# Block 2's mixing stages: TensorE issues in the order of the program

## The chip, the cores and the metric

The kernel runs on one core of a Trainium2 chip. The metric is the device time of one execution in microseconds (us), and the median of several executions is given. A core has five engines that matter here, each with a queue of its own that it works through in order: TensorE (PE in the profile; its weight loads stand apart as PEld), VectorE (DVE), ScalarE (ACT), GpSimd (POOL) and SyncE (SP), which issues the DMA transfers.

## The reference

Two blocks are computed, one behind the other. Block 1 is a diffusion-type transformer on 512 latent and 256 context tokens. Block 2 takes 512 tokens of width 1024 through two layers. What matters here is the first half of each of these layers, the mixing: the normalised input is projected once into many parts, three kinds of mixing run on these parts, their results are put side by side and projected back.

```python
for l in range(DEPTH):
    hn = rms_norm_2(h, attn_norm[l])
    proj = hn @ w_in[l]
    p_a = proj[..., :RW_IN]
    p_b = proj[..., RW_IN:RW_IN + RET_IN]
    p_c = proj[..., RW_IN + RET_IN:]
    ...
    y_a, v_first = rwkv7_mixer(p_a, ...)
    y_b = retention_mixer(p_b, positions)
    y_c = mla_mixer(p_c, positions, mla_q_norm[l], mla_kv_norm[l], mla_w_q_up[l], mla_w_kv_up[l])
    mix = jnp.concatenate([y_a.astype(h.dtype), y_b.astype(h.dtype), y_c.astype(h.dtype)], axis=-1)
    h = h + mix @ w_out[l]
```

- RWKV: four heads of width 64 in two pairs, a recursion over the tokens with data-dependent decay. The kernel computes it in chunks of 64 tokens: inside a chunk a triangular system is solved by doubling, and a state is handed on from chunk to chunk. The output is normalised per head and multiplied by a gate.
- MLA: causal softmax attention of eight heads with keys and queries of width 96 (64 plus 32 with rotary position), whose queries, keys and values come from normalised low-rank latents.
- Retention: four heads of width 64 in two pairs, causal with a fixed decay per head, in chunks of 128 tokens, normalised per head and multiplied by a gate.

A SwiGLU follows as the second half of the layer. Products of projections are made from three matmuls each, on a high and a low part (`whi`, `wlo`; `hh`, `hl`) of both operands.

## The kernel before, in words

The kernel is written as a Python program whose calls append instructions, in the order in which they are made, to the queues of the engines. That is the order of the source. A build step then plans each engine's queue anew: it simulates the engines with estimated costs, and an engine takes whichever of its instructions is ready first. So the order of issue on an engine can differ from the source, wherever nothing that an instruction needs stands against it. A call `tc.keep_in_program_order(ins)` binds an instruction to the one appended just before it on the same engine, so that the build can't exchange the two.

Block 2's mixing (`block2`, L1881 to L1898) has two parts per layer.

The weave. `rwkv` is a Python generator that yields a number whenever the next instruction of its own has to wait for another engine: the gap in microseconds that other work could fill. `weave` adds gap / `STEP` (1.4) to a credit and takes one step of a second generator, the filler, for every whole credit. A filler step is a few matmuls of a projection (six matmuls, two of the eight input tiles times three products), or the vector work behind one. The filler is `mla_inputs` (projections that MLA needs; L1588) and behind it `ret_inputs` and `retention` (L1557, L1689), of which `mla_inputs` itself takes some steps. Two places are of interest: `scale` in `mla_inputs`, which sums squares over tokens with eight small matmuls on a tile `acc` (`token_sums`), and `head_rstd_steps` (L1196 to L1220), which ends each RWKV pair and each retention pair. It does eight small matmuls on squares, then a chain of small VectorE instructions for one over the root (`rsqrt`, L225 to L230, on a tile `smlR` or `smlL`), yields 3.2, and then does sixteen small matmuls that spread the result over rows. Behind it L1552 to L1554 finish the pair on VectorE, and the result is stored.

MLA. When the weave is through, `mla` (from L1893 on) handles eight heads of four query blocks. It casts queries and keys into `qk` (L1770, ScalarE; L1771, VectorE), makes scores, softmax, transposes and products with the values. After each block it takes steps of what is left of the filler, at a rate that spreads them over the stage. What is still left at its end is run at L1895. MLA's pool of tiles takes the place of RWKV's, which is closed by then. Behind the mixing stage come the output products on `mh` and `ml`.

All matmuls go through `mm` (L159) and all transposes through `turn` (L163), so these two lines are TensorE's lines in the profile, and one goes by the tiles' names.

Of the kernel before, what the change touches and what calls it, by code (L numbers as in the profile page):

```python
# [39 lines left out]
class Seg:  # L40


    def __init__(self, key, off, n):
        self.key, self.off, self.n = key, off, n
        self.v = 0 if key == "lat" else 1
# [12 lines left out]
class Kern:  # L58
    def __init__(self, tc, d, out, ctx, V):
        self.tc, self.nc, self.d, self.out = tc, tc.nc, d, out  # L60
        self.ctx, self.V = ctx, V
        nc = self.nc
        self.uid = 0
        E = ctx.enter_context
        self.const = E(tc.tile_pool(name="const", bufs=1))
        self.wp = E(tc.tile_pool(name="wp", bufs=2))
        self.tmp = E(tc.tile_pool(name="tmp", bufs=2))
        self.dram = E(tc.tile_pool(name="dram", bufs=1, space=DRAM))
        c = self.const
        self.vec = c.tile([128, d["vec"].shape[1]], F32, name="vec")  # L70
        nc.sync.dma_start(out=self.vec, in_=d["vec"])
        self.cf = c.tile([128, d["cf"].shape[1]], F32, name="cf")
        nc.sync.dma_start(out=self.cf, in_=d["cf"])
        self.ident = self.cf[:, 0:128]
        self.ones = self.cf[:, 128:129]
        self.bones = self.cf[:, 129:131]
        self.nhalf = self.cf[:, 131:139]
        self.identb = c.tile([128, 128], BF16, name="identb")
        nc.vector.tensor_copy(self.identb, self.ident)
        self.mge = c.tile([128, 128], BF16, name="mge")  # L80
        self.mle = c.tile([128, 128], BF16, name="mle")
        for o, m in ((0, self.mge), (128, self.mle)):
            t = self.tm(128)
            nc.sync.dma_start(out=t, in_=d["cm"][:, o:o + 128])
            nc.vector.tensor_copy(m, t)
        self.ahead = []
        self.banks = {}
        self.lo = "vector"
        self.lb = itertools.cycle("lb")
        self.pend = []  # L90
        self.stream = "L"


    def pool(self, es, name, side=None):
# [61 lines left out]
        self.nc.vector.tensor_tensor(lo, x, hi.bitcast(F32), op=ALU.subtract)  # L156

    def mm(self, out, l, r, start, stop):
        self.nc.tensor.matmul(out, l, r, start=start, stop=stop)  # L159

    def turn(self, out, x):

        self.nc.tensor.transpose(out, x, self.ident)  # L163

    def proj(self, chunks, H, seg, ps):
        for _ in self.proj_steps(chunks, H, seg, ps):
# [1421 lines left out]
    def mla_inputs(self, l, pool, H, bc, rs, tab, dst, acc, bl, other):  # L1588
# [70 lines left out]
        for j in range(2):  # L1659
            yield from latent("kv", 16, 2, j)  # L1660
        turn = rotary()
        next(turn)
        rl = scale("kv", 2)
        yield
# [157 lines left out]
    def block2(self):  # L1822
# [28 lines left out]
        for l in range(2):  # L1851
# [3 lines left out]
            with ExitStack() as es:  # L1855
                es_l = ExitStack()
                self.psum(es, r=4)
                self.psum(es_l, "right", l=2, b=2)
                rp = self.pool(es, "rw")
                bc, slots = X["lat"][7], X["lat"][:7]  # L1860
                ahead = [self.w2proj(l, 6, H)]
                st = self.token_sums(accs, "r")
                rs = self.inv_sqrt(st[:, 0:4], 1.0 / 1024)
                if l == 0:
                    s2 = self.sml(4)
                    nc.vector.tensor_tensor(s2, st[:, 4:8], rs, op=ALU.mult)
                    nc.vector.tensor_tensor(s2, s2, rs, op=ALU.mult)
                    r2 = self.inv_sqrt(s2, 1.0 / 1024)
                    r1, rs = rs, self.one(self.const, [128, 4], F32, "rst")
                    nc.vector.tensor_tensor(rs, r1, r2, op=ALU.mult)  # L1870
                ahead += [self.w2proj(l, j, H) for j in (2, 3)]
                self.spread(rs, "r", bc)
                r, k, v, mis = self.rw_inputs(l, rp, H, bc, slots, ahead)
                es_r, es_rets, es_mix, es_ps = (ExitStack() for _ in range(4))
                retp = self.pool(es_r, "ret", "right")
                mix = [{"lat": [None] * KD} for _ in range(2)]
                with ExitStack() as er:
                    self.order_w(self.orders(l))
                    self.filler = self.counted(self.streamed("L", self.retained(l, retp, es_rets, H, bc, rs, tab_r, mix)))
                    first = self.streamed("L", self.mla_inputs(l, self.pool(er, "fill", "right"), H, bc, rs, tab_m, sm, *self.acc2, self.filler))  # L1880
                    self.weave(self.streamed("R", self.rwkv(l, rp, r, k, v, mis, mixd, vf, C2)), itertools.chain(first, self.filler))  # L1881
                    self.run(first)
                self.lo = "vector"
# [6 lines left out]
            with ExitStack() as es:  # L1890
# [2 lines left out]
                self.mla(l, self.pool(es, "mla"), slots, sm, mixd)  # L1893
                self.stream = "L"
            self.run(self.filler)  # L1895
            es_rets.close()
            es_r.close()
            es_ps.close()  # L1898
# [11 lines left out]
            if l == 0:  # L1910
                b1 = self.bank()
                self.spread_into(r1, b1)
                for k_ in range(KD):
                    x = X["lat"][k_]
# [254 lines left out]
```

## Time and profile before

| what | value |
|---|---|
| median of 3 runs | 3359.4 us (3358.96 to 3359.47) |
| the profiled execution | 3356.98 us |
| its span in the trace | 3355.1 us |
| mixing stage of layer 0 | 1968.4 to 2213.2 us, MLA from 2118.0 |
| mixing stage of layer 1 | 2673.9 to 2920.5 us, MLA from 2832.5 |

The profiled execution is 2.4 us under the median, and 1.9 us of it lie around the span. A timeline gives, for each group of like instructions of one engine, the start, the duration, engine, line, operation, tiles (out<-in), sizes, and in brackets the idle time before it and what ended that. The granted clock of TensorE stands in windows as PEclk; 1.00 is 2.4 GHz.

### The profile page before, as it was taken

To read this page: it belongs to the slowest core of one execution; us is meant where nothing else is said; L and a number is where in the kernel's file an instruction comes from. 1 tells how busy PE (TensorE), PEld (TensorE's weight loads), DVE (VectorE), ACT (ScalarE), POOL (GpSimd) and SP (SyncE) were. 2 spreads that over 40 slices of the span, in tenths; PEclk is the share of its full clock that TensorE was granted. 3 is DMA by queue.
4 is the path that set the end of the run, shared out by engine and by line. 5 is a ranking of instruction groups with operands and counts; after the bars stand their busy time and mean duration, and the time that the engine had idled before them with its cause. 6 is when DMAs were issued, how large, how long until landed. Compare 5 with 4: busy or idle time off the path is not lost. (4 is left out here: it accounts for less than half of the span.)

```text
span 3355.1 us, 48877 instructions
## 1 busy us (share of the span) xinstructions
PE 3281.4 (98%) x19412; PEld 2737.1 (82%) x19412; DVE 1923.1 (57%) x3336; ACT 1233.3 (37%) x2192; POOL 398.6 (12%) x362
## 2 busy tenths in 40 slices
PE   8999999999999999999999999999999999999998
PEld 4888888888888888888888877778888867788887
DVE  7667765666444567757333466774434566754343
ACT  3566632421212346734222432542222332632222
POOL 4231100100000101101000211121101101121001
PEclk8999999999999999999999999999999999999999
DMA  6433373334434243353232323433233323422332
GB/s 217 133 111 123 113 255 128 107 121 135 128 120 133 81 135 101 97 182 118 94 91 98 123 70 103 131 97 94 90 99 98 105 76 102 130 94 94 90 99 82
DMA packets 137533, 385.86 MB, mean 115 GB/s; under 512 B 17428, under 2 KB 29204, under 8 KB 137304
## 3 DMA queue, kind: packets, MB, share of 16 engines
q1 hardware_dynamic: 133976, 372.15, 35.3%
q0 software_dynamic: 3328, 10.57, 1.0%
q8 instruction: 153, 2.51, 0.3%
q14 instruction: 76, 0.62, 0.1%
HBM read 331.56 MB, written 43.76 MB: 112 GB/s over the span
## 5 line engine op out<-in xcount | busy, mean ns | idle before, releaser
L140 ACT CAST whi<-raw 128x1024 fp32r<-128x1024 f32 (+4 forms) x432 | 434.8, 1008 | 1266.7 <-PE b L159 836.1
L141 DVE TENSOR_TENSOR wlo<-raw,whi 128x1024 fp32r<-128x1024 f32 (+4 forms) x427 | 509.2, 1193 | 379.7 <-ACT whi L140 358.2
L159 PE MATMUL b<-hh,whi 128*128 128x512 f32 (+1 forms) x1760 | 686.5, 390 | 0.0
L159 PE MATMUL b<-hl,whi 128*128 128x512 f32 (+1 forms) x1760 | 682.1, 388 | 0.8 <-POOL hl L251 0.8
L159 PE MATMUL b<-hh,wlo 128*128 128x512 f32 (+1 forms) x1760 | 681.7, 387 | 0.0
L159 PEld LDWEIGHTS b<-hh,whi 128*128 128x128 f32 x1760 | 331.0, 188 | 75.5 <-issue 4.8
L159 PEld LDWEIGHTS b<-hh,wlo 128*128 128x128 f32 x1760 | 330.8, 188 | 73.7 <-issue 0.7
L159 PEld LDWEIGHTS b<-hl,whi 128*128 128x128 f32 x1760 | 331.0, 188 | 71.5 <-POOL hl L251 1.2
L159 PE MATMUL b<-ah,whi 128*128 128x512 f32 (+1 forms) x864 | 316.8, 367 | 0.0
L159 PE MATMUL b<-al,whi 128*128 128x512 f32 (+1 forms) x864 | 316.5, 366 | 0.0
L159 PE MATMUL b<-ah,wlo 128*128 128x512 f32 (+1 forms) x864 | 316.3, 366 | 0.0
L159 PEld LDWEIGHTS b<-ah,whi 128*128 128x128 f32 x864 | 163.1, 189 | 28.2
L159 PEld LDWEIGHTS b<-ah,wlo 128*128 128x128 f32 x864 | 163.0, 189 | 28.0
L159 PEld LDWEIGHTS b<-al,whi 128*128 128x128 f32 x864 | 163.1, 189 | 27.8
L948 DVE TENSOR_TENSOR tm<-tm,b 128x512 f32<-128x512 f32 (+1 forms) x112 | 70.0, 625 | 198.8 <-PE b L159 192.8
L409 DVE SCALAR_TENSOR_TENSOR wlo<-raw,silb 128x1024 f32<-128x1024 f32 x128 | 157.6, 1232 | 45.3 <-DMA raw<-in_ada1b 24.5
L159 PE MATMUL l<-hh,whi 128*128 128x512 f32 (+1 forms) x472 | 176.7, 374 | 0.7 <-DVE stB L698 0.3
L159 PE MATMUL l<-hl,whi 128*128 128x512 f32 (+1 forms) x472 | 173.5, 368 | 0.0
L159 PE MATMUL l<-hh,wlo 128*128 128x512 f32 (+1 forms) x472 | 172.9, 366 | 0.0
L509 DVE TENSOR_TENSOR pt<-t,pt 128x384 fp32r<-128x384 f32 (+2 forms) x272 | 131.0, 511 | 36.5 <-ACT pt L508 34.9
L159 PE MATMUL b<-hc,whi 128*128 128x256 f32 x800 | 141.5, 279 | 0.0
L468 DVE TENSOR_REDUCE st<-S 128x1 f32<-128x768 f32 (+2 forms) x160 | 121.6, 763 | 33.5 <-PE S L159 32.7
(561 smaller groups left out, 5766.2 us busy)
## 6 DMA issues: line engine op xcount, KB each, us to landing
raw<-in_wgu SPq DMA_DIRECT2D x92, 512.0 KB, 3.3
raw<-in_w2gu SPq DMA_DIRECT2D x88, 512.0 KB, 3.4
raw<-in_ada1b SPq DMA_DIRECT2D x48, 512.0 KB, 3.3
raw<-in_w2in SPq DMA_DIRECT2D x38, 512.0 KB, 3.6
raw<-in_ada0b SPq DMA_DIRECT2D x32, 512.0 KB, 3.9
raw<-in_wg SPq DMA_DIRECT2D x32, 512.0 KB, 3.4
raw<-in_w2d SPq DMA_DIRECT2D x32, 512.0 KB, 3.5
raw<-in_wd SPq DMA_DIRECT2D x24, 512.0 KB, 3.5
```

The source lines that it names most:

```text
L140: self.nc.scalar.copy(hi, raw)
L141: getattr(self.nc, self.lo).tensor_tensor(lo, raw, hi.bitcast(F32), op=ALU.subtract)
L159: self.nc.tensor.matmul(out, l, r, start=start, stop=stop)
L409: nc.vector.scalar_tensor_tensor(junk, raw, 0.5, self.silb[:, v], op0=ALU.mult, op1=ALU.mult, accum_out=m[:, w, k, v:v + 1])
L468: nc.vector.tensor_reduce(nm, S[:, lo:hi], axis=AX.X, op=ALU.max, negate=True)
L509: nc.vector.tensor_tensor(o, src, h.bitcast(F32), op=ALU.subtract)
L948: nc.vector.tensor_tensor(b, th, pu, op=ALU.mult)
```

## The change

For the length of both mixing stages, every matmul and transpose is bound to the one appended before it: TensorE's queue is the source's order from the weave on until the last step of filler behind MLA. The switch `given` is off everywhere else. The other engines' queues are still planned by the build.

```diff
@@ class Kern, __init__ @@
         self.stream = "L"
+        self.given = False
@@ mm, turn @@
     def mm(self, out, l, r, start, stop):
-        self.nc.tensor.matmul(out, l, r, start=start, stop=stop)
+        self.queued(self.nc.tensor.matmul(out, l, r, start=start, stop=stop))
 
     def turn(self, out, x):
 
-        self.nc.tensor.transpose(out, x, self.ident)
+        self.queued(self.nc.tensor.transpose(out, x, self.ident))
+
+    def queued(self, ins):
+
+        if self.given:
+            self.tc.keep_in_program_order(ins)
@@ block2, each layer @@
                     first = self.streamed("L", self.mla_inputs(l, self.pool(er, "fill", "right"), H, bc, rs, tab_m, sm, *self.acc2, self.filler))
+                    self.given = True
                     self.weave(self.streamed("R", self.rwkv(l, rp, r, k, v, mis, mixd, vf, C2)), itertools.chain(first, self.filler))
                     self.run(first)
...
             self.run(self.filler)
+            self.given = False
             es_rets.close()
```

## Rows read from the trace of the kernel before

**Rows 1.** The page: span, and busy time of each engine.

```profile
span 3355.1 us, 48877 instructions
...
PE 3281.4 (98%) x19412; PEld 2737.1 (82%) x19412; DVE 1923.1 (57%) x3336; ACT 1233.3 (37%) x2192; POOL 398.6 (12%) x362
```

**Rows 2.** Windows: weave, hand-over and end of MLA, both layers.

```profile
core 0: us, PE busy (x) PEld busy (x) DVE busy (x) ACT busy (x) POOL busy (x), PEclk, DMA share, GB/s
1968.40:2118.00 149.60, 143.91 (x1588) 108.87 (x1587) 102.67 (x272) 41.74 (x74) 16.98 (x22) 0.97 0.28 82
2118.00:2145.50 27.50, 25.58 (x181) 21.67 (x180) 22.54 (x43) 15.37 (x38) 5.13 (x4) 1.00 0.38 113
2174.40:2213.20 38.80, 35.22 (x305) 28.44 (x303) 27.73 (x81) 22.36 (x60) 6.61 (x6) 0.96 0.42 130
2673.90:2832.50 158.60, 149.42 (x1602) 111.44 (x1601) 105.14 (x275) 44.73 (x77) 21.50 (x25) 0.97 0.27 81
2832.50:2861.30 28.80, 28.23 (x211) 24.61 (x209) 21.66 (x48) 16.30 (x41) 4.26 (x4) 1.00 0.38 117
2884.40:2920.50 36.10, 32.97 (x304) 27.22 (x301) 27.22 (x81) 22.07 (x60) 6.47 (x6) 1.00 0.44 140
```

**Rows 3.** Timeline of TensorE: token sums, layer 0, then layer 1.

```profile
2052.40 0.40 PE L159 MATMUL b<-hh,whi 128*128 128x512 f32 x1
...
2053.57 0.40 PE L159 MATMUL b<-hh,wlo 128*128 128x512 f32 x1
2054.88 1.05 PE L159 MATMUL b<-cf,acc 128*128 128x1 f32 x8 [0.91 <-DVE acc L208]
...
2698.63 1.05 PE L159 MATMUL b<-cf,acc 128*128 128x1 f32 x8 [1.48 <-DVE acc L208]
```

**Rows 4.** Timeline of TensorE: hand-over of layer 0.

```profile
2117.97 0.40 PE L159 MATMUL b<-hh,whi 128*128 128x512 f32 x1
...
2122.36 1.09 PE L159 MATMUL r<-cf,smlR 128*64 128x128 f32 x16 [0.49 <-DVE smlR L230]
...
2129.97 0.48 PE L159 MATMUL l<-qk,qk 96*128 96x128 f32 x2
```

**Rows 5.** Timeline of VectorE and ScalarE: hand-over of layer 0.

```profile
2116.66 0.17 DVE L1207 TENSOR_SCALAR smlR<-r 128x8 f32<-128x8 f32 x1 [2.74 <-PE r L159]
...
2122.06 0.15 DVE L230 SCALAR_TENSOR_TENSOR smlR<-smlR,smlR 128x8 f32<-128x8 f32 x1
2123.50 0.75 DVE L1552 SCALAR_TENSOR_TENSOR s<-s,vec,r 128x512 f32<-128x512 f32 x1 [1.28 <-PE r L159]
...
2125.07 0.69 DVE L1554 TENSOR_TENSOR s<-s,r 128x512 f32<-128x512 f32 x1
...
2128.77 1.13 ACT L1770 CAST qk<-x 96x512 fp32r<-96x512 f32 x2
```

**Rows 6.** Timeline of TensorE: hand-over of layer 1.

```profile
2832.49 0.39 PE L159 MATMUL b<-hh,whi 128*128 128x512 f32 x1
...
2836.32 1.09 PE L159 MATMUL r<-cf,smlR 128*64 128x128 f32 x16
```

**Rows 7.** Windows: two of the stretches at a lower granted clock.

```profile
2079.20:2082.60 3.40, 3.40 (x12) 2.69 (x9) 2.14 (x5) 0.00 (x0) 0.86 (x3) 0.50 0.56 130
2922.30:2929.10 6.80, 6.48 (x14) 4.74 (x15) 4.55 (x6) 2.33 (x5) 1.55 (x1) 0.50 0.24 77
```

**Rows 8.** Timeline: end of layer 0's MLA, VectorE and TensorE.

```profile
2205.25 0.17 DVE L1202 TENSOR_TENSOR smlL<-b,r 128x8 f32<-128x8 f32 x1 [1.22 <-PE b L159]
...
2208.77 1.05 PE L163 MATMUL t<-cf,x 128*128 128x128 f32 x4 [0.92 <-ACT x L472]
...
2209.42 0.17 DVE L1210 TENSOR_TENSOR smlL<-smlL,rst 128x8 f32<-128x8 f32 x1
...
2211.87 1.34 PE L159 MATMUL o<-mpt,mv 128*128 128x256 f32 x8
```

**Rows 9.** Timeline of TensorE: first products behind each mixing stage.

```profile
2215.30 0.97 PE L159 MATMUL b<-mh,whi 128*128 128x512 f32 x3 [1.15 <-ACT mh L155]
...
2922.61 0.79 PE L159 MATMUL b<-mh,whi 128*128 128x512 f32 x1 [2.14 <-ACT mh L155]
```

## The prediction

> **What bounds the kernel now.** I read the page first. It gives the span, and TensorE (PE) as busy for nearly all of it, with VectorE (DVE) at 57% and every other engine below that [rows 1]. So the time is the time of TensorE's queue: work on other engines costs only where TensorE waits for it, and a wait that nothing fills is paid in full. The edit acts in Block 2's two mixing stages (1968.4 to 2213.2 us and 2673.9 to 2920.5 us), so I cut these into three stretches each, by windows: the weave, the hand-over to MLA, and the end of MLA [rows 2]. The reader is to see there how much TensorE idles: 149.60 − 143.91 = 5.69 us and 158.60 − 149.42 = 9.18 in the weaves, 27.50 − 25.58 = 1.92 and 28.80 − 28.23 = 0.57 at the hand-overs, 38.80 − 35.22 = 3.58 and 36.10 − 32.97 = 3.13 at the ends. Whatever order is used there, the most that better cover could win is 24.1 us.
>
> Then I read TensorE's timeline of both stages against the order of the source. It is nearly the source's own order already: only some fifty places in about 1,540 instructions of a layer differ. The change matters at those alone, and most of them are of one kind: filler that the build put ahead of an instruction that waits for another engine. I took them in turn.
>
> **The change, part by part.** It removes and adds no instruction, no transfer and no semaphore that a result needs. It fixes the order in which TensorE issues; the other engines' queues are still planned, against that order.
>
> *Token sums* (`scale`, called twice a layer). The eight small matmuls on `acc` wait for VectorE's sum of squares. Before, filler of the projection that follows was moved ahead of them: in layer 0 six matmuls, from 2052.40 to 2053.57, and even so the sums still waited 0.91 us [rows 3]. The other three places have 2, 8 and 6. They are spaced by (2053.57 − 2052.40) / 5 = 0.234 us. In source order they stand behind the sums, so the wait is longer by their time: 22 × 0.234 = **5.1 us**. VectorE's `acc` comes no sooner for it, since nothing before it has moved. The bounds are 0, if the planner brings L208 forward, and 5.1.
>
> *Hand-over, first wait.* `head_rstd_steps` of the second RWKV pair traces eight sums on TensorE, a chain of twelve small VectorE operations, `yield 3.2`, and then sixteen small matmuls (L1218) on the chain's result `smlR`. By the source the 3.2 of credit buys two filler steps, and the second is a rope without matmuls: six matmuls stand in between. The six are through at 2117.97, and from there to 2122.36 before ran sixteen matmuls of filler that the source places in MLA [rows 4]. In source order this filler is not there, and TensorE waits for `smlR`, which is written at 2122.06 + 0.15 [rows 5]: 2122.36 − 2117.97 = 4.39 us. In layer 1 the same stretch is 2836.32 − 2832.49 = 3.83 us [rows 6]. The low bound: twelve operations at about 0.2 us each (start to start, as from 2116.66) make 2.4 us, so if VectorE ran nothing between them the wait would be about 1.1 us. The planner ranks VectorE's queue by the same estimates as before, so I keep the measured chain.
>
> *Hand-over, second wait.* Behind those sixteen the next TensorE instructions of the source are MLA's first scores, and these need `qk`. Before, over fifty filler matmuls stood there, to 2129.97 [rows 4]. Now the chain is: L1552 to L1554 on VectorE, from 2123.50 to 2125.07 + 0.69 = 2125.76; they are the last to use RWKV's pool, whose place the MLA pool takes; then ScalarE's two casts, 1.13 us [rows 5]: first scores at about 2126.9. The sixteen end near 2123.4, so the wait is 3.5 to 3.6 us, and the same in layer 1. If the casts also had to wait until the store of `s` has landed, 2 to 3 us more per layer; if the pools do not overlap, nothing.
>
> So the hand-over gains 4.39 + 3.6 = 8.0 and 3.83 + 3.6 = 7.4 us of waits, against 1.92 and 0.57 that it has now and that go into them: 6.1 + 6.9 = **13.0 us** (bounds 4 and 19).
>
> *Clock.* There are six stretches in the two stages and just behind them in which the granted clock is 0.50, the lower of its two levels (1.2 GHz); the first and the last are [rows 7]. They are 3.4 or 6.8 us long, three of each, and each comes after waits of TensorE. Half of such a stretch is lost: 2.55 us in the mean. Each hand-over will now have two waits of about 4 us close together, where before it ran at 1.00 [rows 2]. I take one stretch for each: **5.1 us** (bounds 0 and 10). The Trainium skill ("TensorE: Matmul & The Clock Gate", section "Loop structure matters more than you think") speaks against the change here: matmuls should follow one another while the other engines' work is overlapped, and a wait between matmuls lets the clock fall. The trace agrees, with 0.50 behind the 2.14 us wait of [rows 9]; by that rule the term stays, and without it the sum would be 5.1 us less.
>
> *End of MLA.* Retention's two norms go through the same function on the last filler. In source order only about 2.1 us (first) and 0.65 us (second) of TensorE work, by the durations that these instructions have in the trace, lie between its sums and its sixteen matmuls, and the VectorE chain takes from 2205.25 to 2209.59 [rows 8]: 4.3 us, with other work between its operations, or 14 × 0.2 = 2.9 without. That gives waits of about 2.0 and 2.9 us, and the last eight matmuls on values (1.34 us [rows 8]) lose the sixteen as cover: 1.3 more, 6.2 us per layer. Something is won here, though: the stretch's own idle goes into it, save 1.90 of 3.58 and 0.56 of 3.13 that wait for ScalarE whatever the order (0.92 of it is in [rows 8]), and the next stage's wait for `mh` (1.15 and 2.14 us) [rows 9] is worked off meanwhile. So 6.2 − 1.68 − 1.15 = 3.4 and 6.2 − 2.57 − 2.14 = 1.5: **4.9 us** (bounds −5 and 12).
>
> *Inside RWKV.* The doubling levels and the state recursion keep the places they have, and the few filler matmuls that change sides of a hop do it both ways: 0 (bounds −2 and +3).
>
> The sum: 5.1 + 13.0 + 5.1 + 4.9 = 28.1 us. On the profiled execution's 3357.0 that is 3385.1; this execution lies 2.4 us under the median of the runs, so the median comes to 3387.5. I write **3387 us**.
>
> **The rivals.** 0.2% (6.7 us) is about what a measurement can tell from no change.
>
> *Heavier.* The first scores also wait for the landing of RWKV's store, the half clock lasts 6.8 us at each hand-over or comes back at the ends, and the end's terms are near their upper bound: 13.0 goes to 18, 5.1 to 8, 4.9 to 9, in all some 40 us, **3400**. For it: casts into `qk` stand at 2128.77, after that landing could have been. Against it: nothing in the page shows which of the two they waited for.
>
> *No measurable change.* The waits come, but the planner, seeing TensorE stand at `smlR` and at `qk`, puts VectorE's chain and the casts first: 2.4 us of chain leaves 1.1 instead of 4.4, casts start at once, the clock stays up, and the end's gain (−5) pays for the rest: 5.1 + 4 + 0 − 5 = 4 us, **3364**. Against it: in both layers VectorE ran filler's work between the chain's operations, and nothing in the edit ranks that work lower.
>
> *Faster.* Mechanism: filler that before ran early is missing later, and in source order it stands in the hops of RWKV and at MLA's end for which it was written. Its price at full effect: the weaves' idle 5.69 + 9.18 = 14.9, their four stretches at half clock 10.2, and the avoidable end waits 1.68 + 1.15 + 2.57 + 2.14 = 7.5, together −32.6. It would have to pay for the token sums and the hand-over, 18.1: net −14.5, **3345**. It decides from 24.8 us, three quarters of the whole, on. For it: half-clock stretches do sit in the weave. Against it: in the weave only 22 matmuls are out of place by more than a hop, so there is hardly any stolen filler to give back.
>
> That the edit does nothing is excluded by the places of [rows 3] and [rows 4], which source order doesn't allow.
>
> **How the numbers follow.** The likeliest case (3372 to 3394) 0.62; heavier (3394 to 3406) 0.17; no measurable change 0.12; faster 0.09. Thus faster 0.09, within 0.2% 0.12, slower 0.79. The range leaves out the faster case and the tail of the heavier: 3360 to 3403; the likeliest case's own is 3372 to 3394.
>
> **What would show it.** In the profile after: the same counts of instructions; TensorE waiting for `smlR` (L230) about 4 us and then for `qk` 3.6 us at each hand-over; the sums on `acc` waiting about 2 us and more instead of 0.91 and 1.48 [rows 3]; a clock below 1.00 in the hand-over windows; a wait for `smlL` at the end and a smaller one for `mh`. I am wrong if TensorE's idle time in the mixing stages grows by less than 10 us, or if the weaves get shorter.

## The result and the profile after

The changed kernel takes 3408.86 us in the median of 4 runs (3405.53 to 3411.57), against 3359.18 (3358.58 to 3359.47): a ratio of 1.014, 95% interval 1.0127 to 1.0152, or +49.7 us. The prediction had the direction and about half the size: +28, and 3387 in a range from 3360 to 3403. The profiled execution took 3411.57 us, 54.6 more than the one of before, and it is the one taken apart here.

In the changed kernel's listing TensorE's matmuls stand at L160 (L159 before) and the other lines of the argument six lines lower: L214 for L208, L236 for L230, L1216 for L1210, L1777 for L1771. The page gives the same counts of instructions on every engine, so no work came or went (the total in the first line, which also has instructions that are in no engine's count, differs by 15):

```profile
span 3409.8 us, 48862 instructions
...
PE 3293.3 (97%) x19412; PEld 2752.7 (81%) x19412; DVE 1922.5 (56%) x3336; ACT 1233.4 (36%) x2192; POOL 397.7 (12%) x362
```

TensorE's busy time rose by 3293.3 − 3281.4 = 11.9 us [rows 1] with the same matmuls, and the granted clock below is lower. The rest of the 54.7 us of span, some 43 us, is idle time. To see where, I put each matmul of the one trace beside its like in the other and cut the changed kernel's at the same matmuls. By layer, the windows are the weave, the hand-over, the end of MLA, and the first output products behind it. The last cut of layer 1 fell among like matmuls that the two orders place differently, so the tail of MLA stands in the window behind (278 matmuls against 304), and these two windows are to be read together:

```profile
core 0: us, PE busy (x) PEld busy (x) DVE busy (x) ACT busy (x) POOL busy (x), PEclk, DMA share, GB/s
1968.04:2128.13 160.09, 147.87 (x1588) 113.71 (x1586) 103.24 (x271) 41.53 (x73) 17.09 (x22) 0.93 0.26 76
2128.13:2162.67 34.54, 26.42 (x181) 22.57 (x180) 22.05 (x46) 16.16 (x41) 5.13 (x4) 0.90 0.36 105
2191.49:2237.60 46.11, 34.16 (x305) 28.49 (x304) 29.77 (x83) 23.56 (x63) 7.31 (x6) 0.91 0.37 110
2237.60:2258.55 20.95, 20.95 (x83) 16.82 (x83) 11.24 (x18) 5.22 (x9) 1.28 (x1) 0.87 0.16 51
2699.43:2866.22 166.79, 150.77 (x1601) 113.81 (x1599) 106.05 (x274) 45.84 (x79) 20.62 (x25) 0.95 0.26 76
2866.22:2904.02 37.80, 30.85 (x211) 27.10 (x210) 23.10 (x51) 17.70 (x44) 4.11 (x4) 0.86 0.32 98
2928.31:2968.70 40.39, 30.34 (x278) 26.12 (x277) 26.44 (x76) 19.62 (x52) 7.35 (x6) 0.87 0.30 97
2968.70:2998.35 29.65, 26.57 (x105) 20.14 (x104) 10.13 (x17) 9.71 (x19) 1.28 (x1) 0.83 0.25 77
```

Beside [rows 2]: idle time in the weaves is 12.22 and 16.02 us (5.69 and 9.18 before), at the hand-overs 8.12 and 6.95 (1.92 and 0.57), at the ends 11.95 and 10.05 (3.58 and 3.13). That is +13.4, +12.6 and +15.3. The granted clock is below 1.00 in every one of these windows; both hand-overs had 1.00 before. The windows behind the ends had this before:

```profile
2213.05:2232.99 19.94, 18.79 (x84) 14.69 (x84) 13.25 (x19) 6.49 (x11) 2.64 (x2) 1.00 0.18 53
2920.20:2943.66 23.46, 21.31 (x78) 16.27 (x78) 8.30 (x11) 6.81 (x11) 2.73 (x2) 0.85 0.15 46
```

By length, from like matmul to like matmul, the weaves grew by 10.5 and 8.4 us, the hand-overs by 6.9 and 8.8, the ends and what follows them by 8.4 and 10.7. These are 18.9, 15.7 and 19.1 of the 54.7 us; 1.1 lie between hand-over and end.

The timeline of TensorE shows the waits that were forecast by name, first the token sums, then the hand-over, then the end, and then the wait of the next stage:

```profile
2055.14 1.77 PE L160 MATMUL b<-cf,acc 128*128 128x1 f32 x8 [2.32 <-DVE acc L214]
...
2132.71 1.09 PE L160 MATMUL r<-cf,smlR 128*64 128x128 f32 x16 [4.18 <-DVE smlR L236]
...
2137.35 0.69 PE L160 MATMUL l<-qk,qk 96*128 96x128 f32 x2 [3.16 <-DVE qk L1777]
...
2206.51 1.09 PE L160 MATMUL b<-cf,smlL 128*64 128x128 f32 x16 [2.63 <-DVE smlL L1216]
2212.65 0.57 PE L160 MATMUL b<-rv,rkt 128*64 128x64 f32 x12 [1.49 <-DVE rp L1722]
2223.07 1.97 PE L160 MATMUL b<-cf,smlL 128*64 128x128 f32 x16 [3.45 <-DVE smlL L1216]
...
2724.43 1.86 PE L160 MATMUL b<-cf,acc 128*128 128x1 f32 x8 [3.60 <-DVE acc L214]
...
2977.47 0.79 PE L160 MATMUL b<-mh,whi 128*128 128x512 f32 x1 [1.25 <-ACT mh L156]
```

These two sums wait 2.32 and 3.60 us where they waited 0.91 and 1.48 [rows 3]; the sixteen matmuls on `smlR` wait 4.18 (forecast 4.39), and MLA's first scores 3.16 (3.6). The norms at the end wait 2.63 and 3.45 (2.0 and 2.9). Not in the forecast are that the wait for `rp` between these two grew (1.0 us before), and that `mh` is still waited for in layer 1, 1.25 us after 2.14 [rows 9].

Nor were waits inside RWKV. The clearest is that of the matmuls on `tt` in layer 0. The first two lines are from before, where three filler matmuls on `lat`, the first two of them in the first line, stand ahead of the wait; the third is from the changed kernel, where they stand elsewhere:

```profile
2075.86 0.73 PE L159 MATMUL l<-lat,whi 128*128 128x512 f32 x2
2078.18 1.12 PE L159 MATMUL r<-x,tt 64*64 64x32 f32 x32 [0.42 <-DVE tt L1456]
2083.63 1.92 PE L160 MATMUL r<-x,tt 64*64 64x32 f32 x32 [2.45 <-DVE tt L1462]
```

Three of the stretches at half clock, by windows. The first two come right behind one of those waits, the third begins among short waits of the end (0.28 to 0.68 us) and lasts beyond the one for `mh`:

```profile
2055.30:2062.10 6.80, 6.80 (x21) 5.64 (x22) 3.26 (x9) 0.00 (x0) 1.01 (x1) 0.50 0.12 31
2133.80:2140.60 6.80, 3.64 (x10) 2.91 (x11) 3.68 (x6) 0.00 (x0) 0.00 (x0) 0.50 0.37 131
2973.50:2983.80 10.30, 8.87 (x23) 6.60 (x24) 4.47 (x7) 3.44 (x7) 1.28 (x1) 0.50 0.22 53
```

Windows cut at each change of the granted clock give fifteen such stretches in the two stages and just behind them, 92.2 us in all, against six and 30.7 us before [rows 7].

### The profile page after: what moved, and what is told of

Its sections match the earlier page's. It is cut to its first block, busy times and chain, and to the rows that moved or that the text cites. A ratio compares the mean times of both kernels' runs of the same rounds, so it can differ in the third digit from the quotient of the medians.

```text
span 3409.8 us, 48862 instructions
## 1 busy us (share of the span) xinstructions
PE 3293.3 (97%) x19412; PEld 2752.7 (81%) x19412; DVE 1922.5 (56%) x3336; ACT 1233.4 (36%) x2192; POOL 397.7 (12%) x362
## 5 line engine op out<-in xcount | busy, mean ns | idle before, releaser
L160 PE MATMUL b<-hh,whi 128*128 128x512 f32 (+1 forms) x1760 | 690.4, 392 | 0.5 <-ACT whi L141 0.5
L160 PE MATMUL b<-hh,wlo 128*128 128x512 f32 (+1 forms) x1760 | 684.2, 389 | 0.9 <-DVE wlo L142 0.9
L160 PE MATMUL b<-hl,whi 128*128 128x512 f32 (+1 forms) x1760 | 684.5, 389 | 0.4 <-POOL hl L257 0.4
L160 PEld LDWEIGHTS b<-hh,whi 128*128 128x128 f32 x1760 | 333.1, 189 | 76.3 <-issue 4.5
L160 PEld LDWEIGHTS b<-hh,wlo 128*128 128x128 f32 x1760 | 332.6, 189 | 75.3 <-DVE wlo L142 1.4
L160 PEld LDWEIGHTS b<-hl,whi 128*128 128x128 f32 x1760 | 332.8, 189 | 70.8 <-POOL hl L257 0.8
L160 PE MATMUL b<-ah,whi 128*128 128x512 f32 (+1 forms) x864 | 316.8, 367 | 0.0
L160 PE MATMUL b<-al,whi 128*128 128x512 f32 (+1 forms) x864 | 316.5, 366 | 0.0
L160 PE MATMUL b<-ah,wlo 128*128 128x512 f32 (+1 forms) x864 | 316.3, 366 | 0.0
L160 PEld LDWEIGHTS b<-ah,whi 128*128 128x128 f32 x864 | 163.0, 189 | 28.0
L160 PEld LDWEIGHTS b<-ah,wlo 128*128 128x128 f32 x864 | 163.0, 189 | 28.1
L160 PEld LDWEIGHTS b<-al,whi 128*128 128x128 f32 x864 | 163.1, 189 | 27.9
L160 PE MATMUL l<-hh,whi 128*128 128x512 f32 (+1 forms) x472 | 177.5, 376 | 0.8 <-DVE stB L704 0.3
L160 PE MATMUL l<-hl,whi 128*128 128x512 f32 (+1 forms) x472 | 173.9, 369 | 0.0
L160 PE MATMUL l<-hh,wlo 128*128 128x512 f32 (+1 forms) x472 | 172.8, 366 | 0.0
L160 PE MATMUL b<-hc,whi 128*128 128x256 f32 x800 | 141.5, 279 | 0.0
```

Of the source, the lines that this page charges most:

```text
L160: self.queued(self.nc.tensor.matmul(out, l, r, start=start, stop=stop))
```

## The experiments

They ran in four groups, on three chips, each with the kernel before beside it. That kernel has a median of 3360.1 to 3361.0 us in each group of runs, with a wider spread (3352.7 to 3370.8), so ratios with their intervals decide, and shifts between traces show the place. An interval of 0.3% is 10 us, so differences between two of these kernels are good to some 5 us or worse. Line numbers move by a few lines from kernel to kernel; the tiles' names stay.

**By place.** The first four pin a part of the stretch. The first two are shown against the changed kernel.

```diff
 weave only:                                  MLA only:
                     self.given = True        -  self.given = True
                     self.weave(...)
                     self.run(first)
+                    self.given = False       +  self.given = True
```

> Only the weaves are pinned; from MLA on the build plans TensorE's queue again. If the cost adds up by place, as the shift between the two traces says (weaves +10.4 and +8.4 us, hand-overs +6.9 and +8.8, ends and what follows them the rest), this is +19 us, about 3378. My prediction's own terms for the weaves were 5.1 us, 3364. If the places are coupled (a wait early lowers the clock for later ones), clearly more than 3378.

Measured: 3371.96 us, ratio 1.0036 (1.0023 to 1.005): +11.2. The traces' shift in the two weaves is +7.3 and +7.5 us, and under 0.6 at the hand-overs. That is less than expected by place (19), more than my own terms (5.1), and there is no sign that a wait early lowers the clock later.

> Only MLA is pinned, from its first instruction on, so both waits of the hand-over and both ends keep the source's order; the weave is free. Additive by place: +36 us, about 3395. The prediction's terms for these places: 13.0 + 5.1 + 4.9 = 23, 3382.

Measured: 3398.19 us, ratio 1.0108 (1.0089 to 1.0127): +37.5. With the weaves' 11.2 that makes 48.7, against 49.7 for the whole change. So these two parts add up, within intervals of 7.7 to 16.8 and 29.9 to 42.7.

```diff
         for h in range(8):
+            self.given = h > 0     # h > 3 in the run of the ends
...
-                    self.given = True
                     self.weave(...)
```

> Pinned only from MLA's second head on: the hand-over is free, the ends are not. Additive by place: +20 us, about 3379, and no wait for smlR or for the first qk in the trace. The prediction's term for the ends: 4.9, 3364.

Measured: 3405.47 us, ratio 1.0129 (1.01 to 1.0157), so a miss: +44.7 us, no less than with all of MLA pinned, and the hand-over is no cheaper at all. In its trace the two hand-over stretches are 9.8 and 11.0 us longer than before, against 6.9 and 8.8 in the changed kernel. In TensorE's timeline the first wait has gone back to 0.49 us, as before, because sixteen matmuls of filler that weren't pinned went ahead of it. Eight more went ahead of the first scores, where before had 47, and then none was left, since the rest is bound behind the second head:

```profile
2120.24 1.09 PE L160 MATMUL r<-cf,smlR 128*64 128x128 f32 x16 [0.49 <-DVE smlR L236]
...
2125.34 0.49 PE L160 MATMUL l<-qk,qk 96*128 96x128 f32 x2 [1.95 <-ACT qk L1777]
...
2128.57 0.69 PE L160 MATMUL l<-qk,qk 96*128 96x128 f32 x2 [2.56 <-DVE qk L1778]
...
2135.77 0.47 PE L160 MATMUL l<-qk,qk 96*128 96x128 f32 x1 [1.75 <-ACT qk L1777]
```

The waits for casts into `qk` add to 6.3 us here. Filler that is spent on one wait is missing at the next, and parts that are pinned do not add up in general.

> Pinned only from MLA's fifth head on: weaves and hand-overs are free. By place, as the shift of the traces says: ends and what follows them, +8 to +11 us per layer, 3376 to 3382, with waits for smlL of 2.6 and 3.5 us. By my prediction's term (the wait takes over the idle time that is there, and the wait for mh): +5, 3364.

Measured: 3382.19 us, ratio 1.0069 (1.0052 to 1.0086): +22.1 (17.5 to 28.9), as expected by place and over four times my term. What is pinned ahead of the fifth head, the hand-over above all, is then worth 37.5 − 22.1 = 15.4, good to some 9 us. TensorE's waits at layer 1's end, by what was waited for:

```profile
PE b L160 <- DVE smlL L1216: 6.1, 2, 3.4
PE b L160 <- DVE rp L1722: 2.1, 2, 1.3
PE b L160 <- ACT mh L156: 1.4, 1, 1.4
PE o L160 <- DVE mpt L515: 0.8, 3, 0.3
PE t L164 <- ACT rc L487: 0.7, 1, 0.7
PE t L164 <- ACT x L478: 0.7, 2, 0.4
PE o L160 <- ACT mpt L514: 0.7, 1, 0.7
```

(Columns: total us, times, longest.) In the kernel before, the same list is this:

```profile
PE b L159 <- ACT mh L155: 2.1, 1, 2.1
PE o L159 <- DVE smlL L230: 1.1, 1, 1.1
PE b L159 <- DVE rp L1716: 0.8, 1, 0.8
PE o L159 <- DVE smlL L229: 0.6, 1, 0.6
PE t L163 <- ACT rc L481: 0.6, 1, 0.6
```

So the idle time that was there did not all go into the waits for `smlL`: those for `rp` and `rc` stayed or grew, that for `mh` fell by only 0.7, and others of MLA's own chains came on top.

**Which kind of order costs.** Two kernels keep each stream's order but let the build place one stream between the other:

```diff
     def queued(self, ins):
         if self.given:
-            self.tc.keep_in_program_order(ins)
+            key = self.lane or ("L" if self.stream == "L" else "M")
+            prev, self.queue[key] = self.queue.get(key), ins
+            if prev is not None:
+                (bind ins behind prev)
```

> Each stream of the two is bound in its own order (the filler's matmuls behind each other, those of RWKV and MLA behind each other), but the build may place the one between the other as it likes. If the cost is where the filler stands against the other stream, this is the kernel before, but for the token sums, which wait inside the filler's stream: the sums' 5.4 us in the weaves and some half clock behind them, so 3364 to 3370. If it is the order inside a stream, near the changed kernel, over 3390.

Measured: 3371.27 us, ratio 1.003 (1.0021 to 1.004): +11.2, just over the first forecast.

```diff
         def scale(nm, n):
+            self.lane = "S"
             st = self.token_sums([accs[nm]], next(self.lb))
+            self.lane, v = None, self.sml(4)
```

> The same with the token sums in a third lane, so that filler may pass them. By the first theory within 0.2% of the kernel before, 3354 to 3367; what it is below the run without the third lane is the price of the sums.

Measured: 3363.71 us, ratio 1.0008 (0.9998 to 1.0018): no difference that can be told from the kernel before. So some 40 of the 50 us are the place of filler against the other stream, and the token sums, which wait inside the filler's own stream, cost 11.2 − 3.6 = 7.6, good to some 5 us. The traces show the sums' waits as in the changed kernel in the first of the two (2.3 and 3.2 us for the longest) and as before in the second (0.9 and 1.4).

> Pinned in the weaves alone, with the token sums in a lane of their own: what is left is RWKV's hops. If weave and sums add up (11.2 less 7.6), 3362 to 3366; if the hops were free, as I had it, 3359 to 3361; if the sums are not to be had apart from the rest, near 3371.

Measured: 3363.51 us, ratio 1.001 (1.0 to 1.0019): +2.6, at most 6.4 by the interval. Its trace reads more: the weaves are 4.2 and 4.4 us longer than before, idle time in them grew by 8.0 us, and the wait for `tt` in layer 0 is 2.43 us, as in the changed kernel. So the hops are not free; they cost between 2.6 and 8 us. This kernel binds in the same way as the two-stream kernels and shows the changed kernel's wait, so that way of binding does hold an order.

**The clock.**

```diff
+    def heat(self, ps, n):
+        for _ in range(n):
+            self.mm(ps, self.hot[:, :128], self.hot, True, True)
...                              (the same ahead of the token sums and MLA's first scores)
         yield 3.2
         out = []
         for j in range(n):
             ps = self.bank(tag)
+            if self.given and j == 0:
+                self.heat(ps, self.warm.pop(0))
```

> The changed kernel, with matmuls added that compute nothing used (128 x 512, into banks that are overwritten next) in its longest waits: 2 to 15 ahead of the token sums, 17 and 14 ahead of the spreading of smlR, 13 ahead of MLA's first scores, 11 and 14 ahead of the spreading of smlL, at 0.234 us each a little less than the wait. If the missing time is the clock's (some 61 us more at half clock than before), the waits stay as long but the clock stays up, and the time falls by 13 to 30 us, to 3380 to 3396. If it is the waits' own, 3406 to 3412.

Measured: 3402.34 us, ratio 1.012 (1.0101 to 1.0139). That lies between the two forecasts, and its interval overlaps the changed kernel's. The profiled execution is 8 us shorter than the changed kernel's (3403.7 against 3411.6), at the edge of what can be compared between two groups of runs. The waits at layer 0's hand-over are filled, with 0.29 us left of 4.18:

```profile
2127.64 4.01 PE L162 MATMUL r<-hh 128*128 128x512 f32 x17
2131.94 1.09 PE L162 MATMUL r<-cf,smlR 128*64 128x128 f32 x16 [0.29 <-DVE smlR L243]
2132.96 3.25 PE L162 MATMUL l<-hh 128*128 128x512 f32 x13
```

and the clock holds there, by windows of the two hand-overs (layer 1's stays at 0.91):

```profile
2127.40:2161.40 34.00, 32.00 (x211) 26.86 (x210) 22.16 (x46) 15.87 (x41) 5.14 (x4) 1.00 0.37 109
2859.30:2899.00 39.70, 36.53 (x238) 32.36 (x237) 23.38 (x51) 17.57 (x44) 4.05 (x4) 0.91 0.31 94
```

Time at half clock falls from 92.2 to 54.6 us, and the time by 8 of the 18.8 that half of this would be: about 0.2 us for each us. At layer 0's hand-over the clock is up throughout, and the stretch is 34.00 us long instead of 34.54. At layer 1's it is 39.70 us instead of 37.80, with a new wait of 2.6 us for `x`. So the low clock at the hand-overs cost almost nothing that filling gave back. The weaves (+8.0 and +5.3 instead of +10.5 and +8.4) and the ends up to the first product on `mh` (+5.4 and +9.4 instead of +7.4 and +10.9) are where it counts.

> Pinned from MLA's fifth head on, with 11 and 14 matmuls that compute nothing used written into the waits for smlL. If the half clock (31 and 34 us in the two layers against 14 and 17 before) is a main part of the ends' +22, the time falls by 5 to 8 us, to 3374 to 3377; if the waits alone are, 3381 to 3384.

Measured: 3377.82 us, ratio 1.0054 (1.0036 to 1.0071), against 1.0069 for the ends without the added matmuls: −4.4 us, with intervals that overlap. The granted clock of the ends, 0.82 and 0.91 there, is 0.97 and 0.96 here. In the traces the gain stands in layer 0, whose end is 4.5 us shorter; layer 1's is 0.2 us shorter up to the first product on `mh`. The profiled execution itself is 3.3 us longer than that of the ends, by time lost ahead of the mixing stages. So the clock may be some 4 of the ends' 22 us; more than that isn't shown.

**Covering the waits by hand.** Four kernels keep the whole order of the program, and write filler ahead of the waits in the source.

```diff
 e5    next(turn), one step ahead of the first sums   ->  three steps;  one more next(other) ahead of the second
 e6    yield 3.2                                      ->  yield 8.8 (second RWKV pair);  four steps of filler ahead of MLA
 e7    yield 3.2                                      ->  yield 3.2, and two more turns (retention's norms);  RSTEPS 52 -> 56
 e8    all three
```

> The changed kernel, with filler written ahead of the token sums in the source: two more steps (twelve matmuls, 2.8 us) ahead of the first sums of a layer, one more (six, 1.4 us) ahead of the second. If the waits for acc cost what the trace shows (0.65 and 2.32 us, 3.60 and 2.33) and the half clock behind them about 0.2 us for each us of it, 7 to 10 us less than the changed kernel in the weaves. If the filler only leaves a hop of RWKV open in exchange, the same as the changed kernel.

Measured: 3411.63 us, ratio 1.0163 (1.0138 to 1.0189): nothing won, as in the second case. The first sums of each layer now wait 0 and 0.49 us (0.65 and 3.60 in the changed kernel), but the second 4.14 and 4.04 (2.32 and 2.33).

> The changed kernel, with the hand-over covered in the source: the second pair's norm yields 8.8 in place of 3.2 (four filler steps more ahead of the sixteen matmuls on smlR), and four filler steps stand ahead of MLA. If the hand-over costs its two waits, the two hand-over stretches fall from +6.9 and +8.8 us to near 0, and the kernel by 12 to 16. If head 1's transfers or casts come next, as in the kernel pinned from the second head on, the wait only moves and less than 6 us are won.

Measured: 3411.26 us, ratio 1.0153 (1.0138 to 1.0168): nothing won, though the waits for `smlR` are gone and those for the first scores are down to 0.56 us in layer 0 and 2.88 in layer 1. What comes next in layer 0 is this, by ScalarE's timeline:

```profile
2134.99 1.13 ACT L1778 CAST qk<-x 96x512 fp32r<-96x512 f32 x2
2142.76 0.62 ACT L1765 CAST mv<-vf 128x512 fp32r<-128x512 f32 x1 [6.65 <-DMA vf<-mlav]
2143.29 0.36 ACT L479 ACTIVATE x<-l,st 128x128 f32<-128x128 f32 x1
```

and by TensorE's:

```profile
2143.79 0.47 PE L165 MATMUL t<-cf,x 128*128 128x128 f32 x1 [4.28 <-ACT x L479]
```

ScalarE's cast of MLA's values stands in its queue ahead of the first softmax and is idle for 6.65 us before it, which the load of the values ends; the first transposes wait for the softmax. With the filler spent earlier, this transfer is no longer covered.

> The changed kernel, with two more filler turns between the sums and the sixteen matmuls of each of retention's norms (and the rate raised to match), so that one or two query blocks of MLA stand in between. If the waits for smlL (2.63 and 3.45 us in both layers) are the ends' price, 8 to 14 us less. If the second norm then falls behind MLA's last block, its wait stays and less than 6 us are won.

Measured: 3419.03 us, ratio 1.0177 (1.0161 to 1.0192), a miss. The waits for `smlL` fall from 6.1 to 3.6 us in layer 0 and 4.1 in layer 1; waits for `rkt` (3.7 us in layer 0, 0.4 in the changed kernel) and for `x` of L522 (2.7 in each layer) come in exchange.

> All three together. If places add up: the changed kernel less 27 to 40 us, so 3369 to 3382, with what is left in RWKV's hops and the clock. If filler is what is short (each step spent early is missed later), well above that, over 3390.

Measured: 3409.1 us, ratio 1.0147 (1.0132 to 1.0162): no better than the changed kernel, as in the case that filler is short.

A fifth keeps the whole order too and makes the steps smaller:

```diff
-                if i % 2 == 0:
+                if self.given or i % 2 == 0:
                     yield
-STEP = 1.4
+STEP = 0.7
-RSTEPS = 52
+RSTEPS = 76
...
```

> The changed kernel with steps of filler half as large (three matmuls, 0.7 us, and a STEP of 0.7): the same order inside each stream, spread more finely over RWKV's gaps. If the weave's waits come from six matmuls at a time that miss a gap, the weaves lose 5 to 8 us, the kernel 3400 to 3404. If they come from gaps that the source gives no or too little credit, nothing: 3407 to 3412.

Measured: 3430.61 us, ratio 1.0213 (1.0196 to 1.0229). This one says little on what it was meant for: steps that take a whole projection were not halved, so the weave spent more filler for the same credit. It is 22 us slower than the changed kernel. Up to the sixteen matmuls on `smlR` the weaves are 29 and 26 us longer than before, and the waits for `whi` alone are 5.0 and 6.9 us.

**The rest of the ends.**

```diff
+        self.lane = tok and "N"   # retention's sums, and its sixteen matmuls, in a lane of their own
```

> Pinned from MLA's fifth head on, as in the run of the ends, but the sums and the sixteen matmuls of retention's norms go in a lane of their own and may slip behind later work. If the two waits for smlL (6.0 and 6.1 us per layer) with their consequences are the ends' price, most of the +22 us is gone: 3362 to 3368. If the rest of the fixed order costs as much, 3370 to 3378.

Measured: 3383.48 us, ratio 1.0073 (1.0056 to 1.0089), over both forecasts: nothing of the +22 is gone. The build did not use the freedom well: the first norm of layer 0 waits 3.69 us, longer than the 2.63 of the changed kernel, and behind the second, at 0.80 us, a wait of MLA's own chain opens:

```profile
2190.16 1.45 PE L161 MATMUL b<-cf,smlL 128*64 128x128 f32 x16 [3.69 <-DVE smlL L1222]
...
2209.09 1.09 PE L161 MATMUL b<-cf,smlL 128*64 128x128 f32 x16 [0.80 <-DVE smlL L1222]
...
2215.12 1.08 PE L161 MATMUL o<-mpt,mv 128*128 128x256 f32 x4 [3.87 <-DVE x L526]
```

So freeing the norms alone won nothing here: with the rest of the order fixed, the time went to the next chain.

## Why the prediction fell short

*Direction and mechanism: right.* Filler that the build had put ahead of waiting matmuls covered those waits; put back, it leaves them open. The two-stream kernels show it: with the place of filler free and each stream's order kept, all but the sums' share of the +50 us is gone. What failed are sizes: the ends, RWKV's hops and the clock.

*Token sums, 5.1 us: right as a wait.* The four waits grew by 1.9 us in layer 0 and 3.5 in layer 1, 5.4. With the clock behind them the sums cost 7.6 by the medians.

*Hand-over, 13.0 us and 5.1 of clock: right as a whole, 15.4 by the runs in part and 15.7 in the changed kernel's trace.* Idle time grew by 6.2 + 6.4 = 12.6, and both waits stand where they were put: 4.18 and 3.52 us for `smlR`, 3.16 and 3.14 for `qk`. The upper bound, a wait for the landing of RWKV's store, is not needed to explain them.

*Inside RWKV, 0: too low.* Of the 13.4 us that the weaves' idle time grew, 5.4 are the sums'; the other 8.0 are RWKV's hops and the filler's own waits, the clearest the one for `tt` in layer 0, 2.45 us instead of 0.42. Alone the hops cost 2.6 us by the medians (up to 6.4). Filler that had covered a hop and now stands on its other side did not balance out. The count behind this term was also off: TensorE has 2,247 and 2,253 instructions in the two stages, by windows, not about 1,540; and the filler ahead of layer 0's first scores was 47 matmuls, not over fifty.

*End of MLA, 4.9 us: the step that failed most.* Measured alone it is 22.1, and this is 17 of the 21.6 us by which the forecast of 28.1 is short of the 49.7; in the changed kernel's trace it is 19.1. Most of the gross waits were nearly right. I had 9.8 us for `smlL` and 2.6 for lost cover; measured are 12.2 for `smlL` and 2.5 for `mpt`, about what the lost cover was to cost. (For `smlL` I had gone below the chain as measured before: 4.3 us less 2.1 and less 0.65 is 5.9 per layer, and 6.1 came.) What failed is that I took off 7.5 us, because the stretch's own idle time "goes into it" and the wait for `mh` "is worked off meanwhile". Only about 4.0 of it came true: the 2.0 us that TensorE had waited at `smlL` already, and 2.0 of `mh` (from 1.15 to 0 in layer 0, from 2.14 to 1.25 in layer 1). The waits for `rp` and `rc` did not go in; they grew by 1.8 and 1.0 us, and new ones for `ry` and `rkt` add 1.7. So idle time at the ends and behind them grew by 15.1 us in place of 4.9, and TensorE's busy time by 4.0, at the lower clock. A reading that fits is that those chains run through TensorE itself: while it stood at `smlL`, what they depend on stood too, and resumed behind it with its own latencies. No run isolates this.

*Clock, 5.1 us: mis-sized, and in the wrong place.* I gave one stretch to each hand-over and none to any other place. Half clock grew by 61 us, not by 10. It does not cost half of its length, though: at about 0.2 us per us, from the run with added matmuls, it is some 13 us (61 × 0.21) in all, an estimate that fits the 11.9 us that TensorE's busy time grew. At the hand-overs, where I had put it, holding the clock up saved 0.5 us of 34.5 in layer 0 and nothing in layer 1; in the ends it saved about 4. The Trainium skill ("TensorE: Matmul & The Clock Gate", section "Loop structure matters more than you think") spoke for more waits meaning a lower clock, and the traces agree: 92.2 us against 30.7.

Put together from the runs in part: sums 7.6, hops 2.6, hand-overs 15.4, ends 22.1, in all 47.7 of the 49.7 us. The changed kernel's own trace puts more into the weaves and less into the ends: 18.9, 15.7 and 19.1. By it the weaves, forecast at 5.1, are short by as much as the ends. Which split is nearer is open, as the parts carry 3 to 6 us of noise each.

*The rivals.* The heavier one had the size (3400) but not the reason: its main part was the hand-over waiting for a landing. The faster one needed the weaves to get shorter; they got 10.5 and 8.4 us longer. That VectorE would run its chain at once did not happen at `smlR`: its 4.18 us are near the 4.39 of the chain as it ran before, not the 1.1 of a chain without other work between its operations.

Left open is how the ends' 22 us divide further. Freeing the norms alone moved the waits, and filling them bought some 4 us, not clear of noise; a run that frees one by one the other chains there was not made. Nor does a run separate what the other engines' queues, planned anew against the fixed order, add to the cost.

## What to carry to other kernels

Where one engine is busy all the time and a limited amount of filler covers the latencies of several chains, price a fixed order by the whole chain behind each wait, not by the wait alone: covering the first wait of the hand-over brought up the casts, and covering those brought up the load of the values. Idle time that is there may be counted as cover for a new wait only if what ends it is seen to go on meanwhile; here only about 4.0 of 7.5 us did. And an order that is kept inside each stream, with the streams free against each other, cost nothing that could be measured here once the one instruction group that waits inside its own stream had a lane of its own.

## What the runs showed of the hardware

TensorE's half clock cost far less than half of its time here: 38 us less of it went with an execution shorter by 8. In a stretch full of waits, layer 0's hand-over, a clock of 1.00 in place of 0.90 gave 0.5 us of 34.5; in layer 1's, 0.91 in place of 0.86 gave nothing.
